# Seven-product blocks of a decoder trunk: products in another order, sums begun one block earlier, the first stage's block moved from column 1536 to 2048, six tiles instead of four loaded by quarters

## Chip, core and metric

The kernel runs on one core of a Trainium2 chip. A core has five engines that run side by side, each through its own list of instructions in order: TensorE (PE, matrix products and transposes), VectorE (DVE), ScalarE (ACT), GpSimd (POOL) and SyncE (SP, which issues most transfers). They wait for each other by semaphores. The metric is the time of one execution in microseconds (us), less being better.

## What is computed

A hybrid decoder trunk of two layers on 256 tokens of width 1024, in float32. Each layer has a feed-forward part, a mixing part (two kinds of attention and a pooling mixer) and a second feed-forward part. The change touches the feed-forward parts only, four in all. From the reference:

```python
def swiglu(x, w_gate, w_up, w_down):
    return (jax.nn.silu(x @ w_gate) * (x @ w_up)) @ w_down
...
        h = h + 0.5 * swiglu(rmsnorm(h, ffn1_norm[l]), ffn1_w_gate[l], ffn1_w_up[l], ffn1_w_down[l])
```

`w_gate` and `w_up` are 1024 x 2816, `w_down` is 2816 x 1024.

## The kernel before

**Split operands.** Every operand of the weight products is split into `hi` (a copy in the format `F32R`, made by ACT) and `lo` (the rest, by DVE), and a product is three matmuls: hi·hi, lo·hi and hi·lo (`mm3`, L209 to L211). A weight tile is 128 x 4 x 512 numbers (1 MB): SP loads it into a `raw` buffer, ACT casts it to `hi` (L191), DVE subtracts to get `lo` (L192). There are five `raw` buffers and three each of `hi` and `lo`. A load goes out when the `lo` of the buffer's last tile is made.

**A feed-forward part** (`ffn`) runs over blocks of 512 columns of gate and up, named by their first column `c`: 0, 512, 1024, 1536, 2048, and 2560 with 256 columns. A block has four tiles: gate and up, each for two halves of the depth 1024. `gemm_tokens` takes a tile through 24 matmuls (four depths of 128, two halves of the tokens, three parts). Behind a block, ACT computes silu (`sg`) and DVE multiplies (`g`, L482). The transposes of a block's `g` (`turned`, L424, results split to `ghi`, `glo` at L407 and L408) are done in the middle of the next block. At a block's end `ahead()` already loads and splits the first tile of the next.

**The block at column `SEVEN` = 1536** is done otherwise, by class `Seven`: a product of 2 x 2 quarters (two halves of the tokens by two of the depth; two of the depth by gate and up) in seven products instead of eight. For this, sums of quarters are needed: `stream` makes four sums of the tokens' quarters (`uf`, `sf`, `sh`, `sl`) in block 512. `sums` loads three weight quarters (`b12`, `b11`, `b22`) and makes three sums on DVE (L254): `t1`, `t2`, and one over `b12`. `more` loads the fourth quarter, `b21`. `parts` splits a quarter or a sum into `hi` and `lo` (L219 on ACT, L220 on DVE). `product` does 12 matmuls (L274). `run` does the seven products, with a second value of `t1` (L291) among them, and adds their results on DVE (L279). The products are named `p1` to `p7`: `p1`, `p2`, `p3` take the plain quarters `b11`, `b21`, `b22`; `p4` to `p7` take sums. `sums` is called at the end of block 1024, straight before the block of the products.

**In the first feed-forward part of all**, block 1024 also starts `tables`: it fetches the positions (`pr`, by a transfer from ACT's queue) and makes masks, distances and angles from them, mostly small operations on DVE. And the first four tiles are loaded and split in quarters of 128 x 512 (`first` in `wsplit_now`); after each quarter one entry of the list `opening` is run, which loads a slice of x transposed (`u.first(k)`, into `xT`, then `uhi` and `ulo` at L372 and L373), or nothing, or a part of x itself.

**The order on each engine** is not only that of the code: a scheduler takes the instructions in the order of their emission and places them by when it reckons them ready, and buffers are handed out as they come free.

Of the kernel before, what the change touches and what calls it, by code (L numbers as in the profile page):

```python
# [19 lines left out]
P = 128  # L20
# [5 lines left out]
KD = D // P  # L26
# [5 lines left out]
NEG = -1e30  # L32


SEVEN = 1536


C_CQ, C_DQ, C_DK, C_DV, C_P, C_G = 0, 416, 928, 1440, 1952, 2464
# [10 lines left out]
def plan():  # L49

    tiles = []

    def add(name, layer, k, nk, c, nc_):
        tiles.append((name, layer, k, nk, c, nc_))

    def ffn(layer, pre):
        for c in range(0, 2 * DFF, 1024):
            blocks = range(c, min(c + 1024, 2 * DFF), 512)
            order = [(b, k) for k in (0, 4) for b in blocks] if c == 0 else [(b, k) for b in blocks for k in (0, 4)]
            if c == 2 * SEVEN:  # L60
                order = [(c, 0), (c + 512, 0), (c + 512, 4), (c, 4)]
            for b, k in order:
                add(f"{pre}_gu", layer, k, 4, b, 512)
        for half in range(2):
            for k in range(0, KF, 4):
                add(f"{pre}_w_down", layer, k, min(4, KF - k), half * 512, 512)

    for l in range(DEPTH):
        ffn(l, "ffn1")
        for c, n in ((C_CQ, 416), (C_P, 512), (C_DQ, 512)):  # L70
            for k in (0, 4):
                add("w_in", l, k, 4, c, n)
        add("mla_w_uq", l, 0, 2, 0, 768)
        add("ukv", l, 0, 1, 0, 1024)
        for c in (C_DK, C_DV):
            for k in (0, 4):
                add("w_in", l, k, 4, c, 512)
        add("pool", l, 0, 4, 0, 128)
        for half in range(2):
            for i in range(3):  # L80
                for k in (0, 4):
                    add("w_in", l, k, 4, C_G + i * D + half * 512, 512)
        for half in range(2):
            for i in (2, 0, 1):
                add(f"w_branch{i}", l, 0, 4, half * 512, 512)
        for half in range(2):
            for k in (0, 4):
                add("w_out", l, k, 4, half * 512, 512)
        ffn(l, "ffn2")
    return tiles  # L90
# [3 lines left out]
def trunk(ctx, tc, x, xt, positions, wall, small, lamrow, fnorm, out):  # L94
    nc = tc.nc
    offs, off = {}, 0
# [13 lines left out]
    def acc():  # L110
        return pa.tile([P, 512], F32, tag="acc", name="acc")
# [41 lines left out]
    latest = [None]  # L153

    def wraw(spec):
        latest[0] = spec
        raw = wp.tile([P, spec[3], spec[5]], F32, tag="raw", name="raw", bufs=RAWS)
        nc.sync.dma_start(out=raw, in_=wsrc(spec))
        return raw


    opening = []
# [17 lines left out]
    def wsplit_now(spec):  # L180
        latest[0] = spec
        _, _, _, nk, _, n = spec
        raw = wp.tile([P, nk, n], F32, tag="raw", name="raw", bufs=RAWS)
        hi = wp.tile([P, nk, n], F32R, tag="hi", name="hi")
        lo = wp.tile([P, nk, n], F32R, tag="lo", name="lo")
        first = offs[spec] < 4 * P * 2048
        fl = lambda a: a.rearrange("p k n -> p (k n)")
        rawf, hif, lof = fl(raw), fl(hi), fl(lo)

        def split(ks):  # L190
            nc.scalar.copy(out=hif[:, ks], in_=rawf[:, ks])  # L191
            nc.vector.tensor_tensor(out=lof[:, ks], in0=rawf[:, ks], in1=hif[:, ks].bitcast(F32), op=ALU.subtract)  # L192

        if first:

            for k in range(nk):
                nc.sync.dma_start(out=raw[:, k], in_=wsrc(spec)[:, k])
                split(slice(k * n, (k + 1) * n))
                if opening:
                    opening.pop(0)()  # L200
            return hi, lo
        nc.sync.dma_start(out=raw, in_=wsrc(spec))
        step = nk * n // (1 if spec[0].startswith("ffn") else 2)
        for k in range(0, nk * n, step):
            split(slice(k, k + step))
        return hi, lo
# [16 lines left out]
    class Seven:  # L223
# [2 lines left out]

        def __init__(self, xh, xl, specs):
            self.xh, self.xl = xh, xl  # L230
            self.s11, self.s12, self.s22, self.s21 = specs

        def stream(self, uh, ul):

# [11 lines left out]
            nc.scalar.copy(out=g(self.sh), in_=g(sf))  # L246
            nc.vector.tensor_tensor(out=g(self.sl), in0=g(sf), in1=g(self.sh).bitcast(F32), op=ALU.subtract)

        def sums(self):

            self.b12, self.b11, self.b22 = wraw(self.s12), wraw(self.s11), wraw(self.s22)
            self.t1 = big2([P, 4, 512], F32, "t1")
            self.t2 = big([P, 4, 512], F32, "t2")
            sub = lambda o, x, y: nc.vector.tensor_tensor(out=flat(o), in0=flat(x), in1=flat(y), op=ALU.subtract)  # L254
            sub(self.t1, self.b12, self.b11)
            sub(self.t2, self.b22, self.t1)
            sub(self.b12, self.b22, self.b12)
            self.p1 = parts(self.b11)

        def more(self):  # L260
            self.b21 = wraw(self.s21)
            self.p5 = parts(self.t1)

# [13 lines left out]
        def run(self, between):  # L277

            add = lambda o, x, y: nc.vector.tensor_tensor(out=o, in0=x, in1=y, op=ALU.add)  # L279
            tile_ = lambda name: tp.tile([P, 512], F32, tag="U", name=name, bufs=4)  # L280
            a = acc()
            self.product(a, (0, 0), self.p1)
            m1 = tile_("m1")
            nc.scalar.copy(out=m1, in_=a)
            p6 = parts(self.t2)
            d = acc()
            self.product(d, 0, self.p5)
            m5 = tile_("m5")
            nc.scalar.copy(out=m5, in_=d)

            nc.vector.tensor_tensor(out=flat(self.t1), in0=flat(self.b21), in1=flat(self.t2), op=ALU.subtract)  # L291
            between()
            p7 = parts(self.b12)
            b = acc()
            self.product(b, 1, p6)
            p2 = parts(self.b21)
            add(m1, b, m1)
            c = acc()
            self.product(c, 2, p7)
            p3 = parts(self.b22)  # L300
            u3 = tile_("u3")
            add(u3, c, m1)
            self.product(a, (0, 1), p2, True)
            p4 = parts(self.t1)
            add(m5, u3, m5)
            self.product(d, 3, p3, True)
            self.product(c, (1, 1), p4, True)
            ahead()
            c12 = tile_("c12")
            add(c12, d, m1)  # L310
            add(m1, c, m1)
            return (a, c12), (m1, m5)

    def gemm_tokens(specs, xh, xl, n, before=None, tail=1, early=None):

# [98 lines left out]
    def ffn(l, pre, u, following, midway=None):  # L414
# [19 lines left out]
        for c in range(0, DFF, 512):  # L434
# [4 lines left out]
            if c == 0:  # L439

                ps = [[b() for _ in range(2)] for b in (acc, trp)]
                for k0 in (0, 4):
                    for m in range(2):
                        wh, wl = wsplit(spec(m * 512, k0))
                        for k in range(4):
                            for t in range(2):
                                tk = slice(t * P, (t + 1) * P)
                                mm3(ps[m][t], u.xh(k0 + k)[:, tk], u.xl(k0 + k)[:, tk], wh[:, k, :], wl[:, k, :],
                                    k0 + k == 0, k0 + k == KD - 1)
                if opened:  # L450
                    u.squares(0)
                    u.squares(1)
                u.factor()
            elif c == SEVEN:
                rows = seven.run(lambda: turned(*pending))
                ps = [[rows[t][m] for t in range(2)] for m in range(2)]
            elif n == 512:
                ps = []
                for m in range(2):
                    ps.append(gemm_tokens([spec(2 * c + m * 512, k) for k in (0, 4)], u.xh, u.xl, 512))  # L460
                    if m == 0:
                        turned(*pending)
                        if c == SEVEN - 1024:
                            at = 2 * SEVEN
                            seven = Seven(u.xh, u.xl, [spec(at, 0), spec(at + 512, 0), spec(at + 512, 4), spec(at, 4)])
                            seven.stream(u.hi, u.lo)
                    elif c == SEVEN - 512:
                        seven.sums()
            else:
                both = gemm_tokens([spec(2 * c, k) for k in (0, 4)], u.xh, u.xl, 512, lambda: turned(*pending))  # L470
                ps = [[b[:, m * n:(m + 1) * n] for b in both] for m in range(2)]
            if c == SEVEN - 512:
                seven.more()
            elif c != SEVEN:
                ahead()
            g = []
            for t in range(2):
# [478 lines left out]

    u = Norm(0, SM_F1)
    u.first(0)
    opening += [lambda k=k: u.first(k) for k in range(1, KD)] + [lambda: None] * 5
    opening += [lambda t=t, n=n: nc.sync.dma_start(out=h[:, t, n * 512:(n + 1) * 512],  # L960
                                                   in_=x[t * P:(t + 1) * P, n * 512:(n + 1) * 512])
                for n in range(2) for t in range(2)]
# [66 lines left out]
```

## Time and profile before

| | |
|---|---|
| three runs | 1215.90, 1215.93, 1216.41 us; median 1215.93 |
| the profiled execution | 1215.91 us, span of its instructions 1214.1 us |
| granted clock of TensorE, mean | 0.997 |
| busy: PE, DVE, ACT, POOL | 98%, 67%, 50%, 6% of the span |
| matmuls | 5944 |
| HBM read | 210.85 MB, 175 GB/s over the span |
| loads of 1 MB | 184, from issue to landing 4.9 us (median) |

The first feed-forward part takes the first 202 us of the span (its last transposes start at 202.36). The others follow the mixing parts: the second and third lie together between 420 and 810 us, the fourth from about 1020 us to the end. In the lines of the timeline that are shown below, the columns are: start in us, duration in us, engine, line of the code, operation, tiles written<-read, their form, and in brackets how long the engine was idle before and what ended that. Numbers at the end of a tile's name are left out there, so `t` is `t1` or `t2`.

### The profile page before, as it was taken

The page shows a single profiled execution, that of the slowest core. Times are in us where ns is not written, and L with a number is a line of the kernel's source. Part 1 is how long each engine was busy: PE and PEld are TensorE (multiplying, and loading weights), DVE is VectorE, ACT ScalarE, POOL GpSimd, SP SyncE. Part 2 cuts the span into 40 slices and gives each one's busy share as a digit, 9 for nine tenths or more (in the row PEclk, how much of TensorE's full clock was granted, in tenths as well). Part 3 has the DMA queues.
Part 4 walks back from the last instruction along what each step waited for, and adds up shares of the span by engine and source line. Part 5 has one row for each costly group of instructions (what it writes and reads, how often), then busy time and mean ns, then how long its engine had stood idle before and what let it go on. Part 6 is the DMA issues. An engine that isn't in the chain of part 4 may idle for free.

```text
span 1214.1 us, 14960 instructions
## 1 busy us (share of the span) xinstructions
PE 1195.1 (98%) x5944; PEld 1001.1 (82%) x5944; DVE 818.4 (67%) x1118; ACT 603.4 (50%) x786; POOL 68.2 (6%) x126
## 2 busy tenths in 40 slices
PE   9989999999999999999999999999999999999997
PEld 7777888998788888888888888899977888888886
DVE  5798555777756757964457964568686486499553
ACT  6455445446544454643454644455465445546442
POOL 0000000700100000000000000025010000000000
PEclk9999999999999999999999999999999999999999
DMA  9736445325345455465555565543443554545540
GB/s 341 255 109 245 165 171 194 132 105 208 107 170 198 160 184 187 173 222 177 191 188 182 175 217 191 174 151 117 160 149 129 185 187 170 198 170 212 178 152 35
DMA packets 34613, 212.85 MB, mean 175 GB/s; under 512 B 4080, under 2 KB 5488, under 8 KB 10992
## 3 DMA queue, kind: packets, MB, share of 16 engines
q1 hardware_dynamic: 33408, 210.52, 49.4%
q10 hardware_dynamic: 1136, 1.40, 0.4%
q8 instruction: 46, 0.75, 0.2%
q14 instruction: 23, 0.19, 0.0%
HBM read 210.85 MB, written 1.05 MB: 175 GB/s over the span
## 4 chain that ended last, share of the span: by engine, by line
PE 88%; DVE 4%; issue 4%; DMA 2%; ACT 1%; POOL 0%; POOLq 0%; ACTq 0%; SPq 0%; DVEq 0%
PE acc L209 24%; PE acc L210 23%; PE acc L211 23%; PE acc L274 6%; PE o L764 2%; PE tr L424 1%; DMA raw<-wall 1%; PE tr L730 1%; DVE lo L192 1%; PE tr L757 1%; PE tr L209 1%; PE tr L211 1%; PE tr L210 1%; PE tr L719 1%; PE tr L355 1%
## 5 line engine op out<-in xcount | busy, mean ns | idle before, releaser
L192 DVE TENSOR_TENSOR lo<-raw,hi 128x1024 fp32r<-128x1024 f32 (+4 forms) x268 | 427.8, 1610 | 283.2 <-ACT hi L191 283.0
L191 ACT CAST hi<-raw 128x1024 fp32r<-128x1024 f32 (+4 forms) x268 | 357.4, 1356 | 373.8 <-PE acc L211 285.6
L210 PE MATMUL acc<-lo,uhi 128*128 128x512 f32 (+1 forms) x768 | 299.1, 389 | 2.9 <-DVE lo L192 2.9
L209 PE MATMUL acc<-hi,uhi 128*128 128x512 f32 (+1 forms) x768 | 300.6, 392 | 0.0
L211 PE MATMUL acc<-hi,ulo 128*128 128x512 f32 (+1 forms) x768 | 298.2, 388 | 0.0
L210 PEld LDWEIGHTS acc<-lo,uhi 128*128 128x128 f32 x768 | 144.3, 188 | 31.9 <-DVE lo L192 3.6
L209 PEld LDWEIGHTS acc<-hi,uhi 128*128 128x128 f32 x768 | 144.1, 188 | 29.1 <-issue 1.3
L211 PEld LDWEIGHTS acc<-hi,ulo 128*128 128x128 f32 x768 | 144.2, 188 | 28.5
L209 PE MATMUL acc<-hi,ghi 128*128 128x512 f32 x352 | 137.7, 391 | 0.0
L211 PE MATMUL acc<-hi,glo 128*128 128x512 f32 x352 | 137.4, 390 | 0.0
L210 PE MATMUL acc<-lo,ghi 128*128 128x512 f32 x352 | 137.3, 390 | 0.0
L209 PEld LDWEIGHTS acc<-hi,ghi 128*128 128x128 f32 x352 | 66.1, 188 | 13.7
L210 PEld LDWEIGHTS acc<-lo,ghi 128*128 128x128 f32 x352 | 66.1, 188 | 13.6
L211 PEld LDWEIGHTS acc<-hi,glo 128*128 128x128 f32 x352 | 66.1, 188 | 13.6
L749 ACT ACTIVATE e<-e,mx 128x128 f32<-128x128 f32 (+1 forms) x96 | 42.7, 446 | 56.0 <-DVE mx L745 34.1
L209 PE MATMUL acc<-uhi,hi 128*128 128x256 f32 x192 | 55.6, 290 | 0.0
L210 PE MATMUL acc<-ulo,hi 128*128 128x256 f32 x192 | 55.2, 288 | 0.0
L211 PE MATMUL acc<-uhi,lo 128*128 128x256 f32 x192 | 55.0, 288 | 0.0
L338 POOL TENSOR_TENSOR r<-r,mhalf 128x2 f32<-128x2 f32 x6 | 4.2, 703 | 704.9 <-DVE r L337 704.9
L480 ACT ACTIVATE sg<-acc,r 128x512 f32<-128x512 f32 (+1 forms) x44 | 28.3, 653 | 23.7 <-PE acc L211 23.7
L220 DVE TENSOR_TENSOR lo<-raw,hi 128x2048 fp32r<-128x2048 f32 x16 | 36.5, 2284 | 2.4 <-ACT hi L219 2.4
L209 PE MATMUL acc<-hi,y 128*128 128x512 f32 x96 | 37.8, 393 | 0.0
(235 smaller groups left out, 1635.6 us busy)
## 6 DMA issues: line engine op xcount, KB each, us to landing
raw<-wall SPq DMA_DIRECT2D x184, 1024.0 KB, 4.9
raw<-wall SPq DMA_DIRECT2D x10, 512.0 KB, 3.6
raw<-wall SPq DMA_DIRECT2D x18, 256.0 KB, 5.0
raw<-wall SPq DMA_DIRECT2D x4, 832.0 KB, 4.4
raw<-wall SPq DMA_DIRECT2D x2, 768.0 KB, 4.2
xT<-xt SPq DMA_DIRECT2D x8, 128.0 KB, 4.4
h<-x SPq DMA_DIRECT2D x4, 256.0 KB, 5.8
fn<-fnorm ACTq DMA_DIRECT2D x1, 512.0 KB, 4.6
```

The costliest lines, as they stand in the source:

```text
L191: nc.scalar.copy(out=hif[:, ks], in_=rawf[:, ks])
L192: nc.vector.tensor_tensor(out=lof[:, ks], in0=rawf[:, ks], in1=hif[:, ks].bitcast(F32), op=ALU.subtract)
L209: nc.tensor.matmul(ps, lhsT=lh, rhs=rh, start=start, stop=False)
L210: nc.tensor.matmul(ps, lhsT=lh, rhs=rl, start=False, stop=False)
L211: nc.tensor.matmul(ps, lhsT=ll, rhs=rh, start=False, stop=stop)
L220: nc.vector.tensor_tensor(out=flat(lo), in0=flat(x), in1=flat(hi).bitcast(F32), op=ALU.subtract)
L274: nc.tensor.matmul(ps, lhsT=x, rhs=y, start=not onto and k == 0 and n == 0, stop=k == 3 and n == 2, skip_group_check=onto)
L355: nc.tensor.transpose(out=ps[:, (i * 2 + t) * P:(i * 2 + t + 1) * P], in_=h[:, t, k * P:(k + 1) * P], identity=ident)
L424: nc.tensor.transpose(out=ptr[:, (i * 2 + t) * P:(i * 2 + t + 1) * P], in_=g[t][:, (j + i) * P:(j + i + 1) * P], identity=ident)
L480: nc.scalar.activation(out=sg, in_=ps[0][t], func=AF.Silu, scale=r)
L749: nc.scalar.activation(out=e[:, sl], in_=e[:, sl], func=AF.Exp, bias=mx[:, i:i + 1], scale=-(2.0 ** -(hd + 1)) if slope else -1.0, accum_o ...
L764: nc.tensor.matmul(o[:, hd * 64:(hd + 1) * 64], lhsT=eT[:, j * P:(j + 1) * P], rhs=v[:, kt, hd * 64:(hd + 1) * 64], start=(kt == 0), stop= ...
```

## The change

1. `SEVEN` becomes a function: the first layer's first feed-forward part has its seven-block at column 2048, the others at 1536 as before.
2. `sums` moves from the end of the block ahead of the seven-block to that block's start, ahead of its own tiles; `parts(b11)` moves from `sums` to `more`, at that block's end. `stream` stays in block 512.
3. `run` takes the products in the order p1, p5, p2, p6, p3, p4, p7, where it was p1, p5, p6, p7, p2, p3, p4, so that the plain quarters alternate with sums. Results are added in another order, five additions as before. p4 gets an accumulator of its own, and p7 is added onto p6's.
4. Six tiles instead of four are loaded by quarters. The list `opening` is reordered: after the first two quarters nothing, after the third the second slice of x, after the fourth the third and fourth, then one after each.

```diff
-SEVEN = 1536
+def sevens(layer, pre):
+    return (2048,) if (layer, pre) == (0, "ffn1") else (1536,)
...
-            if c == 2 * SEVEN:
+            if c // 2 in sevens(layer, pre):
                 order = [(c, 0), (c + 512, 0), (c + 512, 4), (c, 4)]
...
-        first = offs[spec] < 4 * P * 2048
+        first = offs[spec] < 6 * P * 2048
...
-        def sums(self):
-            self.b12, self.b11, self.b22 = wraw(self.s12), wraw(self.s11), wraw(self.s22)
+        def sums(self, specs):
+            s11, s12, s22, self.s21 = specs
+            self.b12, self.b11, self.b22 = wraw(s12), wraw(s11), wraw(s22)
...
             sub(self.b12, self.b22, self.b12)
-            self.p1 = parts(self.b11)
         def more(self):
+            self.p1 = parts(self.b11)
             self.b21 = wraw(self.s21)
             self.p5 = parts(self.t1)
...
-            p6 = parts(self.t2)
+            p2 = parts(self.b21)
             d = acc()
             self.product(d, 0, self.p5)
             m5 = tile_("m5")
             nc.scalar.copy(out=m5, in_=d)
+            between()
+            p6 = parts(self.t2)
+            self.product(a, (0, 1), p2, True)
             nc.vector.tensor_tensor(out=flat(self.t1), in0=flat(self.b21), in1=flat(self.t2), op=ALU.subtract)
-            between()
-            p7 = parts(self.b12)
+            p3 = parts(self.b22)
             b = acc()
             self.product(b, 1, p6)
...
+            p4 = parts(self.t1)
+            self.product(d, 3, p3, True)
+            p7 = parts(self.b12)
+            c = acc()
+            self.product(c, (1, 1), p4)
+            add(u2, d, u2)
+            self.product(b, 2, p7, True)
+            ahead()
...
             elif n == 512:
                 ps = []
+                if c + 512 in sevens(l, pre):
+                    at = 2 * c + 1024
+                    last = latest[0]
+                    seven.sums([spec(at, 0), spec(at + 512, 0), spec(at + 512, 4), spec(at, 4)])
+                    latest[0] = last
...
-                    elif c == SEVEN - 512:
-                        seven.sums()
...
-    opening += [lambda k=k: u.first(k) for k in range(1, KD)] + [lambda: None] * 5
+    opening += [lambda: None] * 2 + [lambda: u.first(1), lambda: (u.first(2), u.first(3))]
+    opening += [lambda k=k: u.first(k) for k in range(4, KD)] + [lambda: None] * 4
```

Line numbers grow by 3 to 9: the split's `lo` is L192 before and L195 now, the sums L254 and L258, the `lo` of `parts` L220 and L223, `g` L482 and L490, a product's matmul L274 and L278.

How this moves rows on DVE at three places. First, at the end of block 0 of the first part: the quarter splits, the tokens' factor `r`, then `g` and the splits of the following tiles. Before:

```order
L192 TENSOR_TENSOR lo<-raw,hi 128x512 x9
L384 TENSOR_TENSOR r<-ss 128x2
L337 TENSOR_SCALAR r<-r 128x2
L482 SCALAR_TENSOR_TENSOR g<-tr,r,sg 128x512
L192 TENSOR_TENSOR lo<-raw,hi 128x2048
L482 SCALAR_TENSOR_TENSOR g<-tr,r,sg 128x512
L192 TENSOR_TENSOR lo<-raw,hi 128x2048 x4
```

And now:

```order
L195 TENSOR_TENSOR lo<-raw,hi 128x512 x7
L388 TENSOR_TENSOR r<-ss 128x2
L341 TENSOR_SCALAR r<-r 128x2
L195 TENSOR_TENSOR lo<-raw,hi 128x512 x6
L490 SCALAR_TENSOR_TENSOR g<-tr,r,sg 128x512 x2
L195 TENSOR_TENSOR lo<-raw,hi 128x512 x2
L195 TENSOR_TENSOR lo<-raw,hi 128x2048 x3
```

The fifth tile's split, one row of 128x2048 between the two `g`, became four quarters ahead of both, and two of the sixth tile's stand there too.

Second, DVE from the end of block 1024 of the first part on, among the rows of the tables (`ang`, `kk`, `neglam`, `sinq`, `cosq`). Before, the sums (L254) follow the block's last `lo`, and then the splits of the products (L220):

```order
L254 TENSOR_TENSOR t_708<-raw 128x2048
L559 SCALAR_TENSOR_TENSOR ang<-kk,ang 128x32
L578 TENSOR_TENSOR neglam<-le 128x1 x2
L559 SCALAR_TENSOR_TENSOR ang<-kk,ang 128x32
L579 TENSOR_SCALAR neglam<-neglam 128x1 x2
L561 TENSOR_SCALAR ang<-ang 128x32
L408 TENSOR_TENSOR glo<-tr,ghi 128x512 x2
L254 TENSOR_TENSOR t_709<-raw,t_708 128x2048
L564 TENSOR_SCALAR kk<-kk 128x32
L566 TENSOR_SCALAR sinq<-sink 128x32
L254 TENSOR_TENSOR raw<-raw 128x2048
L567 TENSOR_SCALAR cosq<-cosk 128x32
```

Now (the first row is the split of block 1536's first tile):

```order
L195 TENSOR_TENSOR lo<-raw,hi 128x2048
L567 SCALAR_TENSOR_TENSOR ang<-kk,ang 128x32
L586 TENSOR_TENSOR neglam<-le 128x1 x2
L567 SCALAR_TENSOR_TENSOR ang<-kk,ang 128x32
L587 TENSOR_SCALAR neglam<-neglam 128x1 x2
L569 TENSOR_SCALAR ang<-ang 128x32
L412 TENSOR_TENSOR glo<-tr,ghi 128x512 x2
L258 TENSOR_TENSOR t_740<-raw 128x2048
L572 TENSOR_SCALAR kk<-kk 128x32
L574 TENSOR_SCALAR sinq<-sink 128x32
L258 TENSOR_TENSOR t_741<-raw,t_740 128x2048
L575 TENSOR_SCALAR cosq<-cosk 128x32
```

and straight behind these:

```order
L490 SCALAR_TENSOR_TENSOR g<-acc,r,sg 128x512
L258 TENSOR_TENSOR raw<-raw 128x2048
L490 SCALAR_TENSOR_TENSOR g<-acc,r,sg 128x512
L195 TENSOR_TENSOR lo<-raw,hi 128x2048 x3
L412 TENSOR_TENSOR glo<-tr,ghi 128x512 x2
```

The three sums moved behind the split of block 1536's first tile, and ahead of the splits of its other three (the x3), with both `g` of block 1024 among them.

Third, DVE in block 1024 of the second feed-forward part; the numbers are those of the tiles, `lo_3932`, `lo_3978`, `lo_4008` before and `lo_3961`, `lo_4007`, `lo_4037` now being the block's second to fourth tile. Before:

```order
L192 TENSOR_TENSOR lo_3932<-raw_3930,hi_3931 128x2048
L247 TENSOR_TENSOR sl_3825<-sf_3819,sh_3824 128x2048
L482 SCALAR_TENSOR_TENSOR g_3902<-acc_3829,r_3727,sg_3900 128x512
L192 TENSOR_TENSOR lo_3978<-raw_3976,hi_3977 128x2048
L254 TENSOR_TENSOR t1_4042<-raw_4036,raw_4038 128x2048
L192 TENSOR_TENSOR lo_4008<-raw_4006,hi_4007 128x2048
L254 TENSOR_TENSOR t2_4043<-raw_4040,t1_4042 128x2048
L254 TENSOR_TENSOR raw_4036<-raw_4040,raw_4036 128x2048
```

And now:

```order
L195 TENSOR_TENSOR lo_3961<-raw_3959,hi_3960 128x2048
L250 TENSOR_TENSOR sl_3843<-sf_3837,sh_3842 128x2048
L490 SCALAR_TENSOR_TENSOR g_3920<-acc_3847,r_3745,sg_3918 128x512
L258 TENSOR_TENSOR t1_3928<-raw_3922,raw_3924 128x2048
L195 TENSOR_TENSOR lo_4007<-raw_4005,hi_4006 128x2048
L258 TENSOR_TENSOR t2_3929<-raw_3926,t1_3928 128x2048
L258 TENSOR_TENSOR raw_3922<-raw_3926,raw_3922 128x2048
L195 TENSOR_TENSOR lo_4037<-raw_4035,hi_4036 128x2048
```

The first sum moved ahead of the third tile's split, the other two ahead of the fourth's.

More of the change, by code (lines that the diff above doesn't have):

```diff
@@ L223, in trunk, with __init__ @@
     class Seven:
-        def __init__(self, xh, xl, specs):
+        def __init__(self, xh, xl):
             self.xh, self.xl = xh, xl
-            self.s11, self.s12, self.s22, self.s21 = specs
+            self.sh = None
         def stream(self, uh, ul):
@@ L257, in sums, with more @@
             sub(self.b12, self.b22, self.b12)
+        def more(self):
             self.p1 = parts(self.b11)
-        def more(self):
             self.b21 = wraw(self.s21)
@@ L289, in run @@
             nc.scalar.copy(out=m5, in_=d)
+            between()
+            p6 = parts(self.t2)
+            self.product(a, (0, 1), p2, True)
             nc.vector.tensor_tensor(out=flat(self.t1), in0=flat(self.b21), in1=flat(self.t2), op=ALU.subtract)
-            between()
-            p7 = parts(self.b12)
+            p3 = parts(self.b22)
             b = acc()
             self.product(b, 1, p6)
-            p2 = parts(self.b21)
-            add(m1, b, m1)
[L298 to L312, printed above, removed]
+            u2 = tile_("u2")
+            add(u2, b, m1)
+            p4 = parts(self.t1)
[6 more added lines that the diff above has]
+            ahead()
+            c21 = tile_("c21")
+            add(m1, b, m1)
+            add(m5, m1, m5)
+            add(c21, c, m1)
+            return (a, u2), (c21, m5)
     def gemm_tokens(specs, xh, xl, n, before=None, tail=1, early=None):
@@ L453, in ffn @@
                 u.factor()
-            elif c == SEVEN:
+                seven = Seven(u.xh, u.xl)
+                if sevens(l, pre)[0] == 1024:
+                    seven.stream(u.hi, u.lo)
+            elif c in sevens(l, pre):
                 rows = seven.run(lambda: turned(*pending))
@@ L462, in ffn @@
                         turned(*pending)
-                        if c == SEVEN - 1024:
-                            at = 2 * SEVEN
-                            seven = Seven(u.xh, u.xl, [spec(at, 0), spec(at + 512, 0), spec(at + 512, 4), spec(at, 4)])
+                        if c == 512 and not seven.sh:
                             seven.stream(u.hi, u.lo)
-                    elif c == SEVEN - 512:
-                        seven.sums()
             else:
@@ L471, in ffn @@
                 ps = [[b[:, m * n:(m + 1) * n] for b in both] for m in range(2)]
-            if c == SEVEN - 512:
+            if c + 512 in sevens(l, pre):
                 seven.more()
-            elif c != SEVEN:
+            elif c not in sevens(l, pre):
                 ahead()
```

## Prediction

> **What bounds the kernel now.** The page comes first: which engine is full, and over which time.
>
> ```profile
> PE 1195.1 (98%) x5944; PEld 1001.1 (82%) x5944; DVE 818.4 (67%) x1118; ACT 603.4 (50%) x786; POOL 68.2 (6%) x126
> ```
>
> TensorE (PE) is busy for 1195.1 of 1214.1 us, and the change leaves its matmuls as they are: seven products of 12 each in a seven-block, before and after. Only PE's idle time and its clock can be won, so the next view is what PE waited for (total us, times, longest):
>
> ```profile
> PE acc L274 <- DVE lo L220: 4.2, 1, 4.2
> PE acc L210 <- DVE lo L192: 2.9, 2, 1.8
> PE acc L274 <- ACT hi L219: 1.5, 1, 1.5
> ```
>
> All four waits stand in the first feed-forward stage, one of them (1.2) at its very start; the others show in the busy time by stretch (us, then busy us and instructions of PE, PEld, DVE, ACT, POOL, the granted clock, DMA share, GB/s):
>
> ```profile
> 29.60:33.00 3.40, 1.65 (x8) 1.07 (x7) 3.40 (x4) 2.47 (x2) 0.00 (x0) 1.00 1.01 419
> 76.80:95.00 18.20, 12.46 (x52) 9.65 (x51) 18.20 (x15) 9.69 (x9) 0.00 (x0) 0.91 0.21 68
> 95.00:220.00 125.00, 125.00 (x614) 106.38 (x613) 73.89 (x80) 57.22 (x64) 4.52 (x15) 1.00 0.56 200
> 420.00:820.00 400.00, 400.00 (x1888) 335.03 (x1887) 262.50 (x223) 199.27 (x196) 9.85 (x24) 1.00 0.53 184
> 1020.00:1200.00 180.00, 180.00 (x820) 149.13 (x820) 118.46 (x89) 87.54 (x76) 0.70 (x1) 1.00 0.47 166
> ```
>
> PE idles 1.75 us near 30 and 5.74 us in the first seven-block (76.8 to 95), where VectorE (DVE) is busy all 18.20 us and the clock is below 1. In the three later feed-forward stages (420 to 820, 1020 to 1200) PE never waits: there the change can only lose.
>
> **The change part by part.** *First tiles by quarters.* The wait near 30:
>
> ```profile
> 28.99 0.75 DVE L482 SCALAR_TENSOR_TENSOR g<-tr,r,sg 128x512 f32<-128x512 f32 x1 [5.38 <-PE tr L211]
> 29.66 2.28 DVE L192 TENSOR_TENSOR lo<-raw,hi 128x2048 fp32r<-128x2048 f32 x1
> 32.00 0.50 PE L210 MATMUL acc<-lo,uhi 128*128 128x512 f32 x1 [1.75 <-DVE lo L192]
> ```
>
> DVE stood idle 5.38 us for PE, wrote `g`, and only then split the fifth tile, for which PE waited. In the new order the fifth tile's four quarter splits stand ahead of `g`, in that idle time: **−1.75 us**. What is late next is the sixth tile, needed 5.4 us later, so nothing. If the casts came late, one quarter's split (0.6) would be waited for instead.
>
> ```profile
> raw<-wall SPq DMA_DIRECT2D x184, 1024.0 KB, 4.9
> raw<-wall SPq DMA_DIRECT2D x18, 256.0 KB, 5.0
> ```
>
> The page's DMA issues say that a load of 256 KB takes as long to land as one of 1024 KB. The Trainium skill (DMA: Bandwidth & Descriptors, "Rules for kernel authors") advises at least 1 MiB per DMA for full bandwidth, which speaks against cutting two loads into eight. These rows show no longer landing, but do not separate bandwidth from queueing; were the two tiles a microsecond later, the fifth would still be there ahead of PE, and the sum would stand.
>
> *The very start.* Rows of before:
>
> ```profile
> 7.18 1.28 DVE L192 TENSOR_TENSOR lo<-raw,hi 128x512 fp32r<-128x512 f32 x2
> 7.92 0.50 PE L210 MATMUL acc<-lo,uhi 128*128 128x512 f32 x1 [1.18 <-DVE lo L192]
> 9.43 0.39 PE L211 MATMUL acc<-hi,ulo 128*128 128x512 f32 x1
> ```
>
> Three weight quarters now load ahead of the second slice of x. The first split need not queue behind that slice, so PE may resume up to 1.2 us earlier (the wait shown); but the second slice lands two quarters later (2 x 256 KB, 1.2 us at the 419 GB/s above), and its `ulo`, first needed at 9.43, is queued behind two more quarter splits (0.6 each). PE runs without a gap from 7.92, so only the last of these waits counts: between −1.2 and +1.2, and I take **0**, as the two are of a size.
>
> *The first seven-block moves from column 1536 to 2048.* Its waits, PE's rows:
>
> ```profile
> 76.80 0.39 PE L274 MATMUL acc<-hi,uhi 128*128 128x512 f32 x1
> 81.62 0.79 PE L274 MATMUL acc<-lo,uhi 128*128 128x512 f32 x1 [4.21 <-DVE lo L220]
> 84.71 0.40 PE L274 MATMUL acc<-hi,ulo 128*128 128x512 f32 x1
> 93.93 0.50 PE L274 MATMUL acc<-hi,sh 128*128 128x512 f32 x1 [1.53 <-ACT hi L219]
> 508.47 0.39 PE L274 MATMUL acc<-hi,uhi 128*128 128x512 f32 x1
> 508.70 0.39 PE L274 MATMUL acc<-lo,uhi 128*128 128x512 f32 x1
> ```
>
> Away go 4.21 and 1.53. Also, from 81.62 to 84.71 seven matmuls took 3.09 us, where at full clock (0.227 a matmul, the last two rows) they take 1.59: the half clock after the long wait cost 1.50. With the 1.75 above, **−8.99 us** stand to be won.
>
> But the DVE queue that caused the wait remains: the position tables, then the sums.
>
> ```profile
> 61.60 0.30 DVE L528 TENSOR_SCALAR ri<-pr 128x256 int32<-128x256 int32 x1 [2.43 <-DMA pr<-positions]
> 62.15 2.29 DVE L192 TENSOR_TENSOR lo<-raw,hi 128x2048 fp32r<-128x2048 f32 x1
> 70.68 2.28 DVE L254 TENSOR_TENSOR t<-raw 128x2048 f32<-128x2048 f32 x1
> 73.43 1.28 DVE L408 TENSOR_TENSOR glo<-tr,ghi 128x512 fp32r<-128x512 f32 x2
> 74.63 2.28 DVE L254 TENSOR_TENSOR t<-raw,t 128x2048 f32<-128x2048 f32 x1
> 77.00 2.28 DVE L254 TENSOR_TENSOR raw<-raw 128x2048 f32<-128x2048 f32 x1
> 79.28 2.28 DVE L220 TENSOR_TENSOR lo<-raw,hi 128x2048 fp32r<-128x2048 f32 x1
> 83.69 1.40 DVE L482 SCALAR_TENSOR_TENSOR g<-acc,r,sg 128x512 f32<-128x512 f32 x2
> 85.01 2.27 DVE L220 TENSOR_TENSOR lo<-t,hi 128x2048 fp32r<-128x2048 f32 x1
> ```
>
> In the new order the three sums, with two `g` between them, stand ahead of the `lo` of the **second tile of block 1536**, now an ordinary block. From the `lo` that begins at 62.15: 8.53 to 70.68 as before; one more `lo` 2.20 (spacing in a row, 2.28 less its overlap); small table rows 0.55 (73.43 − 70.68 − 2.20); `glo` 1.20; first sum to second 2.37; second to third 2.28, and in it a `g` of 0.66; third sum 2.20; a `g` 0.66; the `lo` itself 2.28. Together 22.93. PE is 1.75 early by now, and so are `g` and the positions load that it releases: the chain starts at 60.40 and ends at 83.33. PE starts block 1536 at 76.80 − 1.75 = 75.05 and needs this `lo` after 25 matmuls: 75.05 + 25 x 0.227 = 80.72. A new wait of **+2.6 us**. Bounds: 0 if positions land 2.6 earlier; 4.4 if they land as late as before.
>
> The wait of 1.75 left the clock at 1.00 (first stretch above), that of 4.21 halved it; 2.6 lies nearer to the first, so I add nothing for the clock (upper end 1.5). The Trainium skill (TensorE: Matmul & The Clock Gate, "Part 1: The HAM clock gate") puts the return to half rate at one idle window of about 3.4 us. By that page 2.6 costs nothing more; a threshold under it would make the sum −4.9. No row here shows a wait between 1.75 and 4.21.
>
> After that the sums are a whole block ahead of their products; the 1.53 wait for `hi` has that block for cover.
>
> *Sums a block ahead, products reordered, in the other three stages.* DVE's rows and a PE row of the second one:
>
> ```profile
> 478.29 2.27 DVE L192 TENSOR_TENSOR lo<-raw,hi 128x2048 fp32r<-128x2048 f32 x1
> 480.49 2.28 DVE L254 TENSOR_TENSOR t<-raw 128x2048 f32<-128x2048 f32 x1
> 482.69 2.28 DVE L192 TENSOR_TENSOR lo<-raw,hi 128x2048 fp32r<-128x2048 f32 x1
> 486.02 0.40 PE L210 MATMUL acc<-lo,uhi 128*128 128x512 f32 x1
> 505.74 2.29 DVE L220 TENSOR_TENSOR lo<-raw,hi 128x2048 fp32r<-128x2048 f32 x1 [0.22 <-ACT hi L219]
> ```
>
> The third tile's split (478.29) ends 5.4 us before PE needs it (486.02). The new order puts one sum (2.20) ahead of it and two more ahead of the fourth's: 5.4 becomes 3.2, and the fourth's 6.5 (482.69 + 2.28, needed 24 matmuls or 5.45 after 486.02) becomes 2.1. The tightest splits are those in the products: the one at 505.74 ends at 508.03, and PE uses it at 508.70, 0.67 to spare. The new order keeps seven splits and moves the additions of 0.6 behind later ones. I take **0**, bounds 0 below (there is no wait to win) and +0.7 a stage above, should the 0.67 be missed by as much again.
>
> The three quarters now hold three of five `raw` buffers for a block; each load is covered by the 2 to 3 us of spare.
>
> **Sum**: −8.99 + 2.6 + 0 + 0 = −6.4 on the profiled execution's 1215.91, the same as the median 1215.93: **1209.5 us**.
>
> **Rivals.** *No new wait*: the second tile's `lo` comes in time. For it: 2.43 us of the chain are an idle wait for positions. Against it: DVE has no other gap from 61.60 on. −8.99 gives 1206.9.
>
> *Positions land as late as before*:
>
> ```profile
> pr<-positions ACTq DMA_DIRECT2D x1, 128.0 KB, 5.6
> ```
>
> That small load took 5.6 us, beside a 1 MB tile issued at the same moment. The waits become 4.4, the last of them 3.5, near enough to 4.21 to halve the clock again (1.5): −3.1, 1212.8.
>
> *The wait only moves*: on top of that the fourth tile of block 1536 is late. Its load needs the buffer that the late `lo` releases at 83.3; it lands 4.9 later, and cast and split (1.9 and 2.3) end at 92.4, 2.7 before PE gets there. Were the landing 4 us longer, 1.3 is added: 1214.1, within 0.2%, about what a measurement of this kernel can tell from no change.
>
> *Slower*: loads in the three later stages. There the fourth tile's load waits for the second's split, with three buffers held; its own split then stands behind all three sums, with the 2.1 us left. The load costs once it lands over 7 us after issue (4.9 + 2.1), and undoes the gain at 2.1 more in each of three stages. At 3 us each: −6.4 + 9 = +2.6, 1218.5. Against it: DMA is half idle there (0.53).
>
> **How the numbers follow.** Forecast (a new wait of 1.5 to 3.5 us) 0.60; no new wait 0.15; positions late 0.13; the wait moves 0.07; slower 0.05. The range 1206.8 to 1212.8 takes in the first three (0.88). Faster by over 0.2% (under 1213.5): 0.88; within 0.2%: 0.07; slower: 0.05.
>
> **What would show it.** In the changed profile: no PE wait near 30; one PE wait in the first stage near 80, on a `lo` of L195 and not of a product, 2 to 3 us long; granted clock 1.00 right after it; no wait in a product of the first seven-block; PE busy for the whole of the other three stages. A wait on L278, or any PE idle in a later stage, makes the argument on spare time wrong; half clock after a wait under 3 us makes the clock term wrong.

## The result and the profile after

The changed kernel takes 1209.49 us (median of four runs, 1208.52 to 1210.84) against 1216.17 of before: ratio 0.9942, 95% interval 0.9930 to 0.9955. Its profiled execution took 1208.78 with a span of 1207.0, 7.1 less than the 1214.1 of before. The page's line of busy time and, from the view of waits, those of PE in the first stage (total us, times, longest):

```profile
PE 1193.4 (99%) x5944; PEld 999.8 (83%) x5944; DVE 818.9 (68%) x1124; ACT 603.4 (50%) x792; POOL 68.2 (6%) x126
```

```profile
PE acc L213 <- DVE lo L195: 2.3, 1, 2.3
...
PE acc L212 <- DVE uhi L376: 0.5, 1, 0.5
...
PE acc L214 <- DVE ulo L377: 0.4, 1, 0.4
```

The last two stand in the first 10 us. Behind them, where before had one wait near 30 and two in the first seven products, one wait is left, on the `lo` of an ordinary block. The same stretches as before, the last one five us shorter, by engine (us, then busy us and instructions of PE, PEld, DVE, ACT, POOL, the granted clock, DMA share, GB/s):

```profile
29.60:33.00 3.40, 3.40 (x17) 2.81 (x16) 3.04 (x5) 2.02 (x2) 0.00 (x0) 1.00 1.01 419
76.80:95.00 18.20, 15.93 (x74) 12.94 (x74) 13.43 (x11) 6.96 (x8) 0.00 (x0) 1.00 0.43 148
95.00:220.00 125.00, 125.00 (x643) 107.41 (x642) 81.15 (x89) 64.07 (x73) 11.61 (x27) 1.00 0.52 181
420.00:820.00 400.00, 400.00 (x1917) 336.31 (x1916) 263.44 (x227) 197.15 (x191) 17.01 (x37) 1.00 0.54 184
1020.00:1195.00 175.00, 175.00 (x795) 145.09 (x794) 114.51 (x85) 83.22 (x71) 0.70 (x1) 1.00 0.46 160
```

PE is full near 30, idle 2.27 us between 76.8 and 95 (5.74 before), at full clock there (0.91 before), and never idle in the later feed-forward stages, as before. The new wait in PE's rows and the chain that ends in it in DVE's (start, duration, instruction, in brackets the idle time ahead of it):

```profile
80.03 0.39 PE L212 MATMUL acc<-hi,uhi 128*128 128x512 f32 x1
82.69 0.50 PE L213 MATMUL acc<-lo,uhi 128*128 128x512 f32 x1 [2.27 <-DVE lo L195]
83.03 0.39 PE L214 MATMUL acc<-hi,ulo 128*128 128x512 f32 x1
```

```profile
59.15 0.29 DVE L536 TENSOR_SCALAR ri<-pr 128x256 int32<-128x256 int32 x1 [2.41 <-DMA pr<-positions]
...
59.70 2.29 DVE L195 TENSOR_TENSOR lo<-raw,hi 128x2048 fp32r<-128x2048 f32 x1
...
80.35 4.48 DVE L195 TENSOR_TENSOR lo<-raw,hi 128x2048 fp32r<-128x2048 f32 x2
```

From 59.70 to the end of the first of the two splits (80.35 + 2.28 = 82.63) the chain lasts 22.93 us, as worked out ahead. It began 0.70 earlier than assumed, and PE came some 0.5 earlier too.

### The profile page after: what moved, and what is told of

Its sections match the earlier page's. It is cut to its first block, busy times and chain, and to the rows that moved or that the text cites. A ratio compares the mean times of both kernels' runs of the same rounds, so it can differ in the third digit from the quotient of the medians.

```text
span 1207.0 us, 14974 instructions
## 1 busy us (share of the span) xinstructions
PE 1193.4 (99%) x5944; PEld 999.8 (83%) x5944; DVE 818.9 (68%) x1124; ACT 603.4 (50%) x792; POOL 68.2 (6%) x126
## 4 chain that ended last, share of the span: by engine, by line
PE 88%; DVE 5%; issue 4%; DMA 2%; ACT 1%; POOL 0%; SPq 0%; POOLq 0%; ACTq 0%; DVEq 0%
PE acc L212 24%; PE acc L213 23%; PE acc L214 23%; PE acc L278 6%; PE o L772 2%; PE tr L428 1%; DVE lo L195 1%; PE tr L738 1%; PE tr L765 1%; PE tr L214 1%; PE tr L212 1%; PE tr L213 1%; PE tr L727 1%; DMA raw<-wall 1%; PE tr L359 1%
## 5 line engine op out<-in xcount | busy, mean ns | idle before, releaser
L195 DVE TENSOR_TENSOR lo<-raw,hi 128x1024 fp32r<-128x1024 f32 (+4 forms) x274 | 428.9, 1580 | 281.9 <-ACT hi L194 281.7
L222 ACT CAST hi<-raw 128x2048 fp32r<-128x2048 f32 x16 | 30.8, 1923 | 20.8 <-PE acc L214 19.9
```

What stands on the lines that cost most here:

```text
L222: nc.scalar.copy(out=flat(hi), in_=flat(x))
```

## The experiments

Each kernel was timed in five rounds beside the kernel before, whose median was 1216.19, 1216.04 and 1216.20 in the three sets of four.

**First tiles alone** (`tiles_only`: before, with the new opening and this line):

```
-        first = offs[spec] < 4 * P * 2048
+        first = offs[spec] < 6 * P * 2048
```

> The kernel before with the first part of the change alone: six first tiles by quarters and the new order of the opening loads; the seven-blocks stay as they were. Theory: the wait of 1.75 near 30 goes, and with it the wait that stands later in the first seven-block is unchanged in length (the position tables that cause it start with PE), so the time falls by 1.75 to 2.3, to 1213.9 to 1214.4. Rival (the quarter loads cost what the earlier splits gain, or the later wait takes the gain back): the time stays within 0.5 of the 1216.2 of before.

Measured: 1214.05, ratio 0.9979 (0.9971 to 0.9988). The theory holds: 2.1 us, and the wait in the first seven products is still there. Its stretches near 30 and in that block:

```profile
29.60:33.00 3.40, 3.40 (x16) 2.81 (x15) 3.40 (x7) 3.09 (x4) 0.00 (x0) 1.00 1.02 419
...
76.80:95.00 18.20, 13.39 (x50) 10.61 (x51) 17.02 (x13) 8.38 (x8) 0.00 (x0) 0.81 0.24 76
```

The clock of 0.81 (0.91 in the profile of before) says that this execution lost more to the half clock, behind a wait of 4.31: the median shows the gain, not this one run (1215.6).

**The move alone** (`move_only`: before, with the first stage's seven-block at 2048 by `seven_at`, the others at 1536, sums still behind the block ahead, products in the old order):

```
-            elif c == SEVEN:
+            elif c == seven_at(l, pre):
```

> The kernel before with one thing changed: in the first feed-forward stage the seven-block stands at column 2048 instead of 1536; its sums are formed at the end of the block before, as they were, and the products keep their order. Theory: the waits of 4.21 and 1.53 and the half clock of 1.50 go and nothing comes in their place, so the time falls by 7.2, to about 1208.9, and the profile shows no wait of PE between 60 and 110 of over 0.3. Rival (any block behind the position tables pays for them): a wait on a split of block 1536 or 2048 remains, and the time falls by 3 to 5, to 1211 to 1213.

Measured: 1211.71, ratio 0.9956 (0.9944 to 0.9968): 4.5 of the 7.2. The theory fails and the rival's number comes: the 4.21 went, but the wait of 1.5 travelled with the block, and in the profiled execution a half clock followed it. PE's rows and the clock around it:

```profile
108.65 0.39 PE L279 MATMUL acc<-hi,uhi 128*128 128x512 f32 x1
110.57 0.50 PE L279 MATMUL acc<-hi,sh 128*128 128x512 f32 x1 [1.54 <-ACT hi L224]
111.30 0.80 PE L279 MATMUL acc<-lo,sh 128*128 128x512 f32 x1 [0.23 <-DVE lo L225]
```

```profile
111.00:112.00 1.00, 0.77 (x3) 0.61 (x3) 1.00 (x2) 0.00 (x0) 0.00 (x0) 0.61 0.00 0
112.00:113.00 1.00, 1.00 (x4) 0.81 (x3) 1.00 (x1) 0.00 (x0) 0.00 (x0) 0.50 0.75 139
113.00:114.00 1.00, 1.00 (x3) 0.75 (x3) 1.00 (x3) 0.00 (x0) 0.00 (x0) 0.50 0.79 336
114.00:115.00 1.00, 1.00 (x4) 0.80 (x3) 1.00 (x2) 0.00 (x0) 0.00 (x0) 0.68 1.00 426
```

So 1.53 was no property of column 1536.

**Sums of the first stage behind block 1536 again** (`late_sums`: the rest as changed):

```
-                if c + 512 in sevens(l, pre):
+                if c + 512 in sevens(l, pre) and (l, pre) != (0, "ffn1"):
...
             if c + 512 in sevens(l, pre):
+                if (l, pre) == (0, "ffn1"):
+                    at = 2 * c + 1024
+                    seven.sums([spec(at, 0), spec(at + 512, 0), spec(at + 512, 4), spec(at, 4)])
                 seven.more()
```

> The changed kernel with one thing undone: in the first stage alone the three sums are formed behind block 1536, not ahead of it. Theory (the wait of 2.27 on the second tile's lo is three sums long in its queue): the wait goes, the time falls by 2.3 against the changed kernel, to about 1207.2, and all runs show a clock of 0.999. Rival 1 (the wait comes from the position tables alone): it stays, and the time is 1209.5. Rival 2 (the products' new order needs the sums early): a wait of 1 to 2 appears inside the seven products, and the time is 1208 to 1209.5.

Measured: 1208.44, ratio 0.9931 (0.9918 to 0.9945). The second rival came: the 2.27 went and a wait of 1.76 stood in the products, so the two places of the sums cost about the same. Its PE row:

```profile
111.53 0.50 PE L278 MATMUL acc<-hi,uhi 128*128 128x512 f32 x1 [1.76 <-ACT hi L222]
```

**The three later stages as before** (`old_later`: sums behind the block, products in the old order there; `run_before` is the old `run`):

```
-                rows = seven.run(lambda: turned(*pending))
+                rows = (seven.run if (l, pre) == (0, "ffn1") else seven.run_before)(lambda: turned(*pending))
```

> The changed kernel with the second part undone in the three later feed-forward stages: there the sums are formed behind the block ahead and the products stand in the order of before; the first stage is as changed. Theory: PE never waited there by either order, so the time is that of the changed kernel within 0.3, 1209.2 to 1209.8. Rival (the order is worth something that the waits don't show, such as matmul pairs that run faster or a clock): the time moves by 1 or more.

Measured: 1208.95, ratio 0.9936 (0.9924 to 0.9949), not to be told from the changed kernel. PE is full in those stages by either order.

**Position tables begun behind block 2048** (`tables_2560`):

```
-            if c == 1024 and midway:
+            if c == 2560 and midway:
```

> The changed kernel with one number changed: the position tables are begun behind block 2048 of the first stage instead of ahead of block 1024, so that none of their work on DVE stands ahead of the three sums. Theory (the wait of 2.27 on the second tile's lo is a queue of positions, tables and sums on DVE): the wait goes, the clock stays at 1.00 around it, and the time falls to 1206.2 to 1206.8 in all runs. Rival 1 (the three sums alone make it late): a wait of 2 or more stays near 82. Rival 2 (the tables make late what stands behind them in their new place): a new wait of 1 to 3 behind block 2560, and 1207.5 to 1209.5.

Measured: 1212.85, ratio 0.9972 (0.9961 to 0.9984). Both halves of a reading came: the wait at 82 is gone, so the tables were part of its queue; and the second rival took more than that back. DVE's rows, and PE's:

```profile
125.46 0.17 DVE L536 TENSOR_SCALAR ci<-pi 128x2 int32<-128x2 int32 x1 [4.80 <-DMA pi<-positions]
...
125.61 0.69 DVE L283 TENSOR_TENSOR m<-m,m 128x512 f32<-128x512 f32 x1
...
127.35 2.28 DVE L195 TENSOR_TENSOR lo<-raw,hi 128x2048 fp32r<-128x2048 f32 x1
129.55 0.75 DVE L490 SCALAR_TENSOR_TENSOR g<-m,r,sg 128x512 f32<-128x512 f32 x1
```

```profile
130.36 1.54 PE L428 MATMUL tr<-ident,g 128*128 128x128 f32 x6 [4.48 <-DVE g L490]
```

DVE stood 4.80 us for the positions with the last additions of the seven products queued behind, and PE's transposes waited 4.48 for the `g` made from them. A half clock followed that as well.

**The long wait of before filled** (`before_filled`: before, with small matmuls on zeros in it):

```
+                    for i in range(36):
+                        nc.tensor.matmul(fill[:, :256], lhsT=idle[:, :P], rhs=idle, start=True, stop=True)
                 rows = seven.run(lambda: turned(*pending))
```

> The kernel before with 36 small matmuls on zeros put in front of the first seven products of the first stage, where PE waits 4.21 us; by the 5.26 that 24 of them take at half clock they last some 3.9 at full clock, so that PE is never idle for long there. They also change the order in which PE's later instructions are issued: no product's first matmul stands any longer among the matmuls of an earlier product. Theory (the long wait halves the clock; the 1.53 wait is that of a first matmul issued too early): the half clock goes (1.50) and the wait of 1.53 as well, the wait itself is only filled; 1212.6 to 1213.2, and the runs lie within 0.7 of each other. Rival 1 (the half clock has another cause): 1214.2 to 1214.8, with half clock after the filling. Rival 2 (the wait of 1.53 has to do with the late sums, not with the order): 1214.2 to 1214.8 with the wait still there and the clock at 1.00.

Measured: 1214.69 (1214.11 to 1216.58), ratio 0.9988 (0.9979 to 0.9996): the number of the two rivals, 1.4 us. The profile has the clock at 1.00 behind the filled wait, so the half clock comes from PE's idleness. (This one execution, at 1215.65, doesn't show the gain: its waits near 30 are 1.45 and 1.37, in place of the one of 1.75.) In place of the 1.53 two waits on `lo` remained, 0.76 and 0.39, although no matmul was issued early (the stretch of the block, then PE's rows):

```profile
76.80:95.00 18.20, 16.97 (x97) 13.64 (x96) 18.20 (x15) 9.73 (x9) 0.00 (x0) 1.00 0.26 80
```

```profile
92.53 0.50 PE L274 MATMUL acc<-lo,sh 128*128 128x512 f32 x1 [0.76 <-DVE lo L220]
95.93 0.50 PE L274 MATMUL acc<-lo,uhi 128*128 128x512 f32 x1 [0.39 <-DVE lo L220]
```

**The opening in its old order** (`start_old`: six tiles by quarters kept; the list `opening` of before).

> The changed kernel with the opening loads in the order of before (eight slices of x first, a weight quarter after each), the six tiles by quarters kept. Theory: the new order of the opening is worth nothing, 1208.6 to 1209.8 as the changed kernel. Rival 1: it gains up to 1.2, and the time is 1210 or more, with a longer wait of PE ahead of 10 us. Rival 2: it costs, and the time is under 1208.2.

Measured: 1208.83, ratio 0.9937 (0.9925 to 0.9950): the new opening is worth nothing that can be measured. The wait near 82 is 2.43 here, and no slice behind it has a clock under 1.00:

```profile
83.25 0.50 PE L213 MATMUL acc<-lo,uhi 128*128 128x512 f32 x1 [2.43 <-DVE lo L195]
```

**The new wait filled** (`filled`: 18 such matmuls ahead of the second tile of block 1536).

> The changed kernel with 18 small matmuls on zeros put in front of the second tile of block 1536 in the first stage, inside the wait of 2.27 (some 1.95 at full clock), so that the real matmuls start when they did. Theory (in about half of its runs the changed kernel loses 1.7 us to a half clock behind this wait, in the others nothing): all runs stand at 1208.3 to 1209.0, clock 0.999. Rival (the spread from 1208.5 to 1210.8 has another cause): two of the five or so stand at 1210 or above again.

Measured: 1208.96 (1208.52 to 1210.06), ratio 0.9941 (0.9927 to 0.9954); of the wait 0.30 is left. Inconclusive. The run of 1210.06 had a mean clock of 0.999 and a span of 1207.1, so what made it late lies outside the span. By their spans the five runs stand together, 1206.7 to 1207.2, where two of the changed kernel's four had 1208.4 and 1209.1. That speaks for the theory, but `start_old`, with its wait unfilled, had no such run among five either (1206.5 to 1207.6).

**Second tile split ahead of the sums** (`split_first`, first stage):

```
                 if c + 512 in sevens(l, pre):
                     at = 2 * c + 1024
+                    if (l, pre) == (0, "ffn1"):
+                        pending_splits[spec(2 * c, 4)] = wsplit_now(spec(2 * c, 4))
                     last = latest[0]
```

> The changed kernel with one thing moved: in the first stage the second tile of block 1536 is split in the program ahead of the three sums instead of behind them, so that its lo stands on DVE behind the first sum and ahead of the other two. Theory (queue on DVE): the wait of 2.27 goes, the third tile's lo then ends at about 84.8, where the changed kernel's third ended, 1 us before PE needs it; no wait takes its place, PE's order is clean, the clock stays: 1206.2 to 1206.8 against 1208.6 of the changed kernel without a clock loss. Rival (the third tile becomes late by as much): a wait of 1 to 2.3 six microseconds further on, 1207.5 to 1209.

Measured: 1206.43 (1205.94 to 1206.65), ratio 0.9914 (0.9900 to 0.9927): the fastest, and its interval lies clear of the changed kernel's. DVE's rows, and the stretch:

```profile
72.50 2.28 DVE L258 TENSOR_TENSOR t<-raw 128x2048 f32<-128x2048 f32 x1
...
74.87 2.29 DVE L195 TENSOR_TENSOR lo<-raw,hi 128x2048 fp32r<-128x2048 f32 x1
...
77.82 2.28 DVE L258 TENSOR_TENSOR t<-raw,t 128x2048 f32<-128x2048 f32 x1
...
80.68 2.28 DVE L258 TENSOR_TENSOR raw<-raw 128x2048 f32<-128x2048 f32 x1
82.88 4.48 DVE L195 TENSOR_TENSOR lo<-raw,hi 128x2048 fp32r<-128x2048 f32 x2
```

```profile
76.80:95.00 18.20, 18.20 (x86) 15.15 (x85) 14.69 (x12) 8.95 (x8) 0.00 (x0) 1.00 0.63 230
```

The same DVE work in another order: the second tile's `lo` ends at 77.16 instead of 82.63, the third's at 85.16, and PE waits for neither.

**Sums between the halves of block 1536** (`sums_mid`, first stage; called where `turned` of the first half is).

> The changed kernel with the three sums of the first stage formed between the two halves of block 1536: half a block ahead of the products instead of a whole one. By its list of instructions the wait of 2.27 has no sum left in front of it, but on PE the first matmul of the sixth product and that of the seventh stand among the matmuls of the fifth again, as where the sums are formed behind the block. Theory (a first matmul that is issued early waits for its own cast with the ready matmuls behind it): a wait on hi of 1.5 to 1.8 inside the products, 1208.0 to 1208.6. Rival (the late sums cause that wait, and half a block ahead is enough): no wait in the products, 1206.2 to 1206.8.

Measured: 1208.53, ratio 0.9932 (0.9919 to 0.9944). The number and the wait of 1.76 are those of the theory, but its reason falls. PE's rows (the fifth product's first matmul, the sixth's, issued early, and the fifth's second), then DVE's:

```profile
109.55 0.39 PE L278 MATMUL acc<-hi,sh 128*128 128x512 f32 x1
111.70 0.50 PE L278 MATMUL acc<-hi,uhi 128*128 128x512 f32 x1 [1.76 <-ACT hi L222]
112.04 0.40 PE L278 MATMUL acc<-lo,sh 128*128 128x512 f32 x1
```

```profile
96.05 2.29 DVE L258 TENSOR_TENSOR raw<-raw 128x2048 f32<-128x2048 f32 x1
...
107.38 2.28 DVE L298 TENSOR_TENSOR t<-raw,t 128x2048 f32<-128x2048 f32 x1
109.58 2.28 DVE L223 TENSOR_TENSOR lo<-raw,hi 128x2048 fp32r<-128x2048 f32 x1
```

The matmuls queued behind the early one need the `lo` that DVE finishes at 111.86, so they were not ready either, and in their own order PE would have waited as long. DVE is late because the sums run there just ahead of the products, the third at 96.05, not at 80.68 as in the kernel above. A late queue of sums on DVE makes this wait; the early matmul only gives it its name.

**First part undone** (`tiles_undone`: four tiles by quarters, old opening).

> The changed kernel with its first part undone: four tiles by quarters and the opening in its old order. Theory (the parts add up, since the wait at 82 moves along with PE): the wait of 1.75 to 2.1 near 30 is back, the wait of 2.27 keeps its length, 1210.4 to 1211.6. Rival (the later wait takes in part of the earlier one): the wait at 82 shrinks to under 1, 1209.0 to 1209.8.

Measured: 1212.28, ratio 0.9965 (0.9952 to 0.9977), five runs from 1211.07 to 1214.13. The parts add up: a wait of 1.76 is back near 30 and the one near 82, now 2.46, about keeps its length. The median is above the range expected, and the profiled run (1214.05) shows why, in PE's rows and in the two slices of 1 us in which the clock fell (the two behind each have 0.50):

```profile
8.04 0.80 PE L213 MATMUL acc<-lo,uhi 128*128 128x512 f32 x1 [1.99 <-DVE lo L195]
...
83.89 0.39 PE L212 MATMUL acc<-hi,uhi 128*128 128x512 f32 x1
86.73 0.80 PE L213 MATMUL acc<-lo,uhi 128*128 128x512 f32 x1 [2.46 <-DVE lo L195]
```

```profile
8.00:9.00 1.00, 0.96 (x2) 0.83 (x3) 1.00 (x3) 0.61 (x2) 0.00 (x0) 0.54 1.02 345
...
86.00:87.00 1.00, 0.27 (x1) 0.27 (x2) 1.00 (x2) 0.00 (x0) 0.00 (x0) 0.79 0.00 0
```

Two waits of 1.99 and 2.46 were each followed by half clock. This run and that of 1214.13 had a mean clock of 0.996, those of 1211.07 and 1211.21 one of 0.999.

**The block not moved** (`no_move`):

```
-    return (2048,) if (layer, pre) == (0, "ffn1") else (1536,)
+    return (1536,)
```

> The changed kernel with its block not moved: the first stage's seven-block stays at column 1536, and its sums are formed ahead of block 1024, where the position tables are. By its list of instructions the lo of the second tile of block 1024 stands on DVE behind the positions, the tables and all three sums. Theory (one queue on DVE): from the landing of the positions at 59.2 some 9.4 us of DVE work (two sums, 4.4; table rows, 2.7; this lo, 2.3) stand ahead of that tile's first use, which PE reaches at about 57.5; a wait of 10 to 12 us and a clock loss of 1.7 to 3.4, against which the wait of 2.27 goes: 1217.5 to 1222, slower than before. Rival (the move only takes away the 4.21 of before): 1212 to 1215.

Measured: 1217.51, ratio 1.0008 (0.9999 to 1.0017): 8 us above the changed kernel, and not to be told from before. The mechanism is the theory's, the wait of 8.70 is shorter than expected. The `lo` ended when it should (66.31 + 2.28 = 68.59; 59.2 + 9.4 = 68.6), by two errors that cancel: DVE began on the positions 2 us earlier than assumed and had 2 us more to do. PE reached the tile 2.4 later than assumed (68.65 − 8.70 = 59.95), and that is what shortened the wait. PE's row and DVE's:

```profile
68.65 0.79 PE L213 MATMUL acc<-lo,uhi 128*128 128x512 f32 x1 [8.70 <-DVE lo L195]
```

```profile
57.25 0.29 DVE L536 TENSOR_SCALAR ri<-pr 128x256 int32<-128x256 int32 x1
...
57.80 2.28 DVE L258 TENSOR_TENSOR raw<-raw 128x2048 f32<-128x2048 f32 x1
...
63.72 2.28 DVE L258 TENSOR_TENSOR t<-raw,t 128x2048 f32<-128x2048 f32 x1
...
66.31 2.28 DVE L195 TENSOR_TENSOR lo<-raw,hi 128x2048 fp32r<-128x2048 f32 x1
```

Sums a block ahead and the position tables in one block cost about all that the rest brings: the change needs its move.

## Why the prediction was right, point by point

**Place and kind of each step** came as written: no wait near 30, one wait near 80 on a `lo` of L195, 2 to 3 us long, full clock behind it in the profile, no wait in the products of the first seven-block, no wait in the other stages. The new wait was put at 2.6 and is 2.27; its chain was exact, its start and PE's need were each a little off. That it is a queue is shown: it goes when the tables leave the queue (`tables_2560`) and when the tile goes ahead of two sums (`split_first`).

**The sum** was 0.7 short on the profiled execution: 6.4 forecast, 7.1 measured. The mis-sized term is the price of a wait, which the prediction took at the length that the profile prints. In PE's rows of after the matmuls around the new wait start at 80.03, 82.69 and 83.03, 3.00 us for two steps that take 0.45 at full rate: lost are 2.55, 0.28 more than the 2.27 printed. A row is printed 0.39 long and the next starts 0.227 behind it in a row of matmuls, so the idle time is counted from a point 0.16 too late; and the step behind the wait takes 0.34 instead of 0.227. The rows of before around two of the waits removed:

```profile
77.02 0.39 PE L274 MATMUL acc<-hi,sh 128*128 128x512 f32 x1
...
92.00 0.40 PE L274 MATMUL acc<-hi,uhi 128*128 128x512 f32 x1
```

From 77.02 to 81.62 are 4.60, less one step 4.37 (4.21 printed); from 92.00 over 93.93 to 94.26 are 2.26, less two steps 1.81 (1.53 printed). The first tiles brought 2.1 by the medians of `tiles_only` (1.5 to 3.5 by its interval; 1.75 printed). With the half clock of 1.50 as forecast: 2.1 + 4.37 + 1.81 + 1.50 − 2.55 = 7.2, against the 7.1 measured; so close an agreement is in part chance, with a term that is known to a microsecond.

**The median** hit the forecast, 1209.49 for 1209.5, partly by luck: two runs at 1208.5 to 1208.8 (mean clock 0.999) and two at 1210.2 and 1210.8 (0.998). The higher two fit one more stretch of half clock, about 1.7 us, but no profile of them was taken; the spans in `filled` speak for it without showing it.

**The clock** step was right in the profiled run by luck, and wrong as a reason. The prediction laid the limit between 1.75 and 4.21 and added nothing at 2.6, and called half clock after a wait under 3 us the sign that this term is wrong. A wait of 2.46 in `tiles_undone` and one of 1.54 and 0.23 in `move_only` were followed by half clock; one of 2.27 in the changed kernel and one of 2.43 in `start_old` were not.

**The 1.53** was expected to go because the sums come a block ahead. That is what the runs show: it stays with late sums wherever the block stands and in either order of the products (`move_only`, `late_sums`, `sums_mid`). Whether early sums would do with the old order of the products was not run: what the new order adds in this stage stays open. And ahead of the block they cost 2.55: in the first stage the early sums, taken alone, bring nothing that can be told from late ones (`late_sums`), and the gain that the runs show is that of the move and the first tiles.

**The terms at nothing**, the opening and the three later stages, are confirmed by `start_old` and `old_later` within what the runs can tell (some 0.2%). The loads by quarters cost no bandwidth that shows: 419 GB/s near 30 before and after.

**The rivals**: positions landing later did not come, nor did late loads in the other stages. A case without any gain existed in a place that the prediction didn't look at: the sums beside the tables (`no_move`), which the move avoids.

## What to carry to other kernels

When work is moved earlier on an in-order engine, list what then stands behind it and when that is needed, and move the most urgent row ahead of it: here one split put ahead of two sums took 2.4 us off the span (1207.0 to 1204.6) with no work saved. Price a wait by the starts of the instructions around it, not by the idle time printed. Before a slow load's consumer is moved, see what is queued behind it on its engine.

## What was not expected of the hardware

The half clock does not follow from the length of one wait. In the profiled executions it came behind waits of 1.54 with 0.23, 1.99, 2.46, 4.21, 4.31, 4.48 and 8.70 us, and not behind others of 1.53, 1.75, 1.76, 2.27, 2.28 (`old_later`) and 2.43. A stretch of it lasted about 3.4 us or a multiple of that: in `move_only`, by the clocks of 0.61 and 0.68 in the first and last of its four slices, from 111.22 to 114.64; by the same reading 6.82 us in `tables_2560` and in `tiles_only`, and 10.24, three times 3.413, in `no_move`.

In `tiles_undone` the clock changed on a grid of such steps. Its two stretches begin at 8.08 and 86.58 (by the clocks of 0.54 and 0.79 in their slices), 78.50 us apart, 23 times 3.413. In the step ahead of each start, in every profile with half clock, PE was busy for at most 1.74 of 3.41 us (`move_only`, 107.80 to 111.22). So a wait of some 2 us may fall into one step or be split between two. That this decides is likely, but not shown: in the executions at full clock no row tells where the steps lie.

The Trainium skill (TensorE: Matmul & The Clock Gate, "Part 1: The HAM clock gate") puts the return to half rate at one idle window of about 3.4 us, with a window that runs freely. The length of a stretch agrees with that window. That only gaps of over 3.4 us matter does not: the runs show half clock behind less than two.
